# Attention blocks in an alternating order, a second bank for the filling, and probabilities turned as float32r

## The chip, the cores and the metric

The kernel runs on one core of a Trainium2 chip. The metric is the time of one execution on the device in microseconds, measured as a median over runs. A core has five engines with queues of their own: TensorE (PE in the profile, with PEld for its weight loads), VectorE (DVE), ScalarE (ACT), GpSimd (POOL) and SyncE (SP, which here issues nearly all DMA transfers). They run beside one another and wait for one another through semaphores. TensorE writes into PSUM, a memory of eight banks of 512 float32 values on each of 128 partitions.

## The reference

One step of a hybrid encoder layer: 1024 new frames of one stream (`x_prompt`) and 32 frames of a running stream with 512 cached frames (`x_sample`), both of width 1024. The input is normalised and projected to ten groups of columns. Two branches follow, causal attention with 16 heads of 64 and a forget bias, and a causal depthwise convolution over 31 frames with a layer norm. Each is gated and projected, the two are mixed by sigmoid gates, and a last projection and the residual close the layer. Everything is float32.

```
h = rmsnorm(x, norm_g)
q, k, v, logf, ga, ua, ub, gb, ma, mb = columns of h @ w_in      # q and k normalised per head
s = q @ k.T + (C[t] - C[s]);  C = cumsum(logf)                   # causal: masked above the diagonal
o = softmax(s) @ v
conv = dwconv(ua * sigmoid(ub)) + b_dw
ya = (o * silu(ga)) @ w_pa
yb = (silu(layernorm(conv)) * silu(gb)) @ w_pb
y = x + (sigmoid(ma) * ya + sigmoid(mb) * yb) @ w_out
```

It returns y for both streams, the new keys, values and log forget gates, and the tail of the convolution's input.

## The kernel before

**Layout.** Activations lie with channels on partitions and frames along the free axis: 1024 + 32 = 1056 columns, worked in three chunks of 352. A projection is computed as float32r products (`mms`, L97): weights and inputs are split into a high and a low part in float32r, and three products, high by high, low by high and high by low, are added in a bank. A tile of 128 output channels takes 3 chunks x 8 slices of the contraction x 3 products = 72 products of 352 columns. ScalarE casts the raw weights to the high part (`split_w`, L91), GpSimd subtracts for the low part (L94).

**Stages.** First the inputs are turned and split while the first projections start; then v, k, q and the two convolution inputs are projected, with the 31 taps of the convolution on VectorE (L258); then the gate ga. From about 591 to 1095 us lies the attention stage, on which every edit bears. After it come the projections of ya, yb and the output.

**The attention stage.** Queries are cut into 8 blocks of 128 frames per head. `Block.scores` (L894) computes the scores of block i against its (i + 1) x 128 keys, in one bank when there are up to 512 keys, in two otherwise (`nb`), with two products a bank: KB by QB (L905; high and low parts packed on 128 partitions) and KA by QA (L906; 68 partitions, with the forget bias in the last four). A product narrower than 256 columns is padded to 256 (`wm`), which touches block 0 alone. VectorE adds the causal mask on the diagonal (L908) and takes the row maximum (L910), ScalarE writes the exponential to a tile P in SBUF and sums the rows (L913), VectorE takes the reciprocal (L915), and GpSimd scales P in place (L916). The score bank is free again when the exponential is done.

`Block.turn` (L918) transposes P in tiles of 128 x 128 on TensorE (L926, 36 tiles a head, 576 in all): a product in which the tile of P is the stationary operand and the identity matrix the moving one, both float32. Up to four tiles share a bank `ptr` from the pool `psT`, and ScalarE or VectorE copies them to the tile pt (L929). When blocks 0 to 3, or 4 to 7, of a head are turned, `values` (L931) multiplies them by V (L940), and ScalarE and VectorE move the result to the tile ot (L945, L946), which is multiplied by the gate ga and stored for every second head.

**Filling.** Between the blocks TensorE works on projections that nothing in the stage needs: 22 chunk groups of gb, ma and mb (`gate_steps`, L747), 528 steps of three products each through one bank of the pool `pq`. ScalarE evacuates a finished chunk to a tile t (L753) and SP stores it (L754). Layer norm sums of the convolution branch (L978) and the blocks of the sample stream (class `Sample`) are fitted in as well.

**What sets the order.** On TensorE the order is that of the code (a manual schedule). The driver loop (from L1017) visits the blocks in the order 0 to 7 of each head; at a block n it issues the scores of block n + 3, the turn of block n, four filling steps, and the values of block n - 2 when they are due:

```
for n, b in enumerate(seq):
    if n + 3 < len(seq):
        start(seq[n + 3])
    ...
        b.turn()
        fill(4 if b.i > 2 or b.head.h != 8 else 0)
    if n >= 2 and pending(seq[n - 2]):
        seq[n - 2].values()
```

On the other engines a scheduler orders instructions; each engine, SP too, works through its own list in order, so an instruction that waits holds all behind it. A tile that is allocated again under its tag waits until the readers of the buffer's last content are done; `bufs` is the number of buffers of a tag. Before: scores have two buffers of two banks, `psT` three banks, the filling one. P has three buffers. The operands of a head, QA, QB, KA and KB, are loaded by SP in one burst of eight transfers (and V for every second head) five blocks ahead of the head's first block (`Head.load`, L767).

## Time and profile before

| what | us |
|---|---|
| median of 3 runs | 1403.2 |
| lowest and highest of them | 1402.51, 1405.59 |
| the profiled execution, as a run | 1405.11 |
| its span (first to last instruction) | 1403.3 |

The profile shows one execution. A row of busy time gives an engine's busy microseconds, its share of the span and its number of instructions. In a row of groups, the line, the engine, the operation and `output<-inputs` are followed by the count, the busy time in us and the mean of one in ns, and then by the engine's idle time just before them and what ended it. A row of the timeline has the start, the duration from the first start to the last end, and the instructions that it joins. Products are pipelined on PE: each row is longer than the distance to the next start, and it is that distance which counts. A row of windows gives the stretch, its length, the busy time of each engine, the granted TensorE clock, the share of the DMA engines and GB/s. A row of waits gives who waited, for whom, the sum in us, how often and the longest.

### The profile page before, as it was taken

What the parts mean: (1) busy time and instruction counts of PE and PEld (TensorE: products, weight loads), DVE (VectorE), ACT (ScalarE), POOL (GpSimd) and SP (SyncE); (2) the same over time, 40 slices, a digit from 0 to 9 for tenths busy, and PEclk for the clock granted to TensorE, in tenths of its full rate; (3) what the DMA queues carried; (4) which work ended last, traced back from release to release, by engine and by line L of the source; (5) the groups of instructions that cost most, each with busy time, mean ns of one, the idle gap of its engine ahead of it and who ended that gap; (6) DMA issues with size and microseconds to landing.
All of it is one profiled execution on the core that took longest, in us unless ns stands there. A gap on an engine that the chain in (4) does not pass through costs nothing.

```text
span 1403.3 us, 23422 instructions
## 1 busy us (share of the span) xinstructions
PE 1390.1 (99%) x8999; PEld 1303.6 (93%) x8999; DVE 866.0 (62%) x1199; ACT 604.2 (43%) x1180; POOL 617.5 (44%) x541
## 2 busy tenths in 40 slices
PE   8999999999999999999999999999999999999999
PEld 7999999999999999998888888878888999999998
DVE  6687787888898998646655656644444497132111
ACT  6322334646464642245454546544554455232100
POOL 2324254557585875343433433232332366254320
PEclk9999999999999999999999999999999999999999
DMA  4242333424342484335545546353532778444431
GB/s 181 92 141 92 119 108 99 160 76 142 106 152 92 138 194 150 111 100 129 148 107 160 146 136 177 101 154 109 155 115 73 276 254 271 143 138 142 150 108 47
DMA packets 102288, 192.77 MB, mean 137 GB/s; under 512 B 17248, under 2 KB 70368, under 8 KB 102176
## 3 DMA queue, kind: packets, MB, share of 16 engines
q1 hardware_dynamic: 102032, 191.21, 44.4%
q8 instruction: 71, 1.16, 0.4%
q14 instruction: 41, 0.34, 0.1%
q10 hardware_dynamic: 144, 0.07, 0.0%
HBM read 125.58 MB, written 65.64 MB: 136 GB/s over the span
## 4 chain that ended last, share of the span: by engine, by line
PE 92%; issue 3%; DVE 2%; ACT 2%; POOL 1%; DMA 1%; SPq 0%; ACTq 0%; POOLq 0%; DVEq 0%
PE pj L102 67%; PE pjv L582 7%; PE po L940 5%; PE ptr L926 4%; PE psS L905 3%; PE psS L906 2%; POOL wl L94 1%; PE pst L698 1%; PE pst L697 1%; PE po L885 0%; DVE y L1082 0%; PE ptx L427 0%; DMA xtok<-xt 0%; ACT xh L429 0%; PE pjs L541 0%
## 5 line engine op out<-in xcount | busy, mean ns | idle before, releaser
L102 PE MATMUL pj<-xh,wh 128*128 128x352 f32 (+2 forms) x1536 | 510.0, 332 | 1.7 <-ACT t L753 1.1
L102 PE MATMUL pj<-xh,wl 128*128 128x352 f32 (+2 forms) x1536 | 494.0, 322 | 1.9 <-POOL wl L94 1.9
L102 PE MATMUL pj<-xl,wh 128*128 128x352 f32 (+2 forms) x1536 | 495.5, 323 | 0.2
L94 POOL TENSOR_TENSOR wl<-raw,wh 128x384 fp32r<-128x384 f32 (+1 forms) x258 | 323.1, 1280 | 258.1 <-ACT wh L91 226.9
L258 DVE SCALAR_TENSOR_TENSOR y<-u,vec_t,y 128x1086 f32<-128x1086 f32 x240 | 382.5, 1594 | 23.7 <-ACT y L255 19.6
L102 PEld LDWEIGHTS pj<-xh,wh 128*128 128x128 f32 x1536 | 289.0, 188 | 10.2 <-ACT t L753 6.6
L102 PEld LDWEIGHTS pj<-xh,wl 128*128 128x128 f32 x1536 | 289.9, 189 | 2.5 <-POOL wl L94 2.2
L102 PEld LDWEIGHTS pj<-xl,wh 128*128 128x128 f32 x1536 | 289.1, 188 | 1.4 <-DVE xl L430 1.2
L916 POOL TENSOR_SCALAR P<-P,nm 128x128 f32<-128x128 f32 (+7 forms) x128 | 107.6, 842 | 283.3 <-DVE nm L915 216.9
L91 ACT CAST wh<-raw 128x1024 fp32r<-128x1024 f32 x86 | 90.1, 1048 | 111.2 <-PE pj L102 80.5
L913 ACT ACTIVATE P<-psS,nm 128x128 f32<-128x128 f32 (+7 forms) x128 | 95.4, 745 | 70.7 <-DVE nm L910 61.5
L910 DVE TENSOR_REDUCE nm<-psS 128x1 f32<-128x128 f32 (+7 forms) x128 | 96.8, 756 | 8.6
L908 DVE TENSOR_TENSOR psS<-psS,cmask 128x128 f32<-128x128 f32 x128 | 38.1, 297 | 100.3 <-PE psS L906 99.3
L929 ACT COPY pt<-ptr 128x512 f32<-128x512 f32 (+3 forms) x128 | 65.0, 508 | 75.8 <-PE ptr L926 75.1
L715 POOL TENSOR_TENSOR ql<-qn,qh 128x352 fp32r<-128x352 f32 (+1 forms) x48 | 66.0, 1374 | 68.0 <-ACT qh L714 54.9
L926 PE MATMUL ptr<-ident,P 128*128 128x128 f32 x576 | 84.2, 273 | 0.0
L940 PE MATMUL po<-pt,V 128*64 128x512 f32 (+1 forms) x384 | 75.8, 530 | 0.0
L926 PEld LDWEIGHTS ptr<-ident,P 128*128 128x128 f32 x576 | 69.1, 140 | 5.6 <-issue 0.4
L582 PE MATMUL pjv<-vwh,xh 128*128 128x260 f32 x256 | 72.5, 283 | 0.0
L582 PE MATMUL pjv<-vwl,xh 128*128 128x260 f32 x256 | 72.4, 283 | 0.0
L582 PE MATMUL pjv<-vwh,xl 128*128 128x260 f32 x256 | 72.3, 282 | 0.0
L905 PE MATMUL psS<-KB,QB 128*128 128x256 f32 (+2 forms) x192 | 70.1, 366 | 0.6 <-ACT t L751 0.6
(200 smaller groups left out, 2237.4 us busy)
## 6 DMA issues: line engine op xcount, KB each, us to landing
raw<-wf SPq DMA_DIRECT2D x88, 512.0 KB
QB<-s_q SPq DMA_DIRECT2D x32, 256.0 KB
KB<-s_k SPq DMA_DIRECT2D x32, 256.0 KB
kT<-qn SPq DMA_DIRECT2D x8, 528.0 KB
s_ga<-t SPq DMA_DIRECT2D x24, 176.0 KB
s_gb<-t SPq DMA_DIRECT2D x24, 176.0 KB
s_ma<-t SPq DMA_DIRECT2D x24, 176.0 KB
s_mb<-t SPq DMA_DIRECT2D x24, 176.0 KB
```

Of the source, the lines that this page charges most:

```text
L91: nc.scalar.copy(wh, raw)
L94: nc.gpsimd.tensor_sub(wl[:, k0:k1, :], raw[:, k0:k1, :], f32(wh[:, k0:k1, :]))
L102: nc.tensor.matmul(ps, a[:, kt, :], b(kt, sl), start=(first and n == 0), stop=(last and n == N - 1))
L258: t = nc.vector.scalar_tensor_tensor(y, u[:, i:i + CW], w, y, op0=ALU.mult, op1=ALU.add)
L582: nc.tensor.matmul(ps[:, :VC], a, b, start=(n == 0), stop=(n == 23))
L715: nc.gpsimd.tensor_sub(ql[:, :n], qn[:, o], f32(qh[:, :n]))
L905: nc.tensor.matmul(ps[:, b, :wm], QB[:, qsl], KB[:, ksl], start=True, stop=False)
L910: nc.vector.tensor_reduce(nm[:, 0:1], ps[:, :nb, :w], axis=AX.XY, op=ALU.max, negate=True)
L913: nc.scalar.activation(P[:, :nk].rearrange("p (b w) -> p b w", b=nb), ps[:, :nb, :w], AF.Exp, bias=nm[:, 0:1], accum_out=nm[:, 1:2])
L916: nc.gpsimd.tensor_scalar(P[:, :nk], P[:, :nk], nm[:, 2:3], 1.0, op0=ALU.mult, op1=ALU.mult)
L926: nc.tensor.transpose(pt[:, 128 * j:128 * j + 128], P[:, 128 * (4 * u + j):128 * (4 * u + j) + 128], ident)
L940: nc.tensor.matmul(po[64 * o:64 * o + 64, q0:], V[:, j + o, hd], p[:, j + o, q0:], start=(j == 0), stop=(j == njb - 2), skip_group_check=True)
```

## The change

The change has these parts:

- **Order.** A head's blocks run in the order 4, 0, 5, 1, 6, 2, 7, 3, so that a big block (two score banks) alternates with a small one (one bank). Scores are issued four blocks ahead in place of three, and values one block behind in place of two.
- **Banks.** Scores have one tile of two banks (tag S) and one of one bank (tag S1) in place of two tiles of two banks. The bank that this leaves is a second one for the filling (`pq2`); `Banks2` alternates between them.
- **Float32r turns.** P is split by size: tag P2 with two buffers for big blocks, P1 with one for small ones. After GpSimd's scaling, SP issues a transfer of P to a new tile R of type float32r (R2 with two buffers, R1 with one), and the turn reads R and an identity of type float32r, and writes the bank as float32r.
- **Padding.** Scores are no longer padded to 256 columns.
- **Loads.** The operands of a head are loaded two transfers a block, from eleven blocks ahead on. V has one buffer and is loaded when the values of blocks 0 to 3 of the head before are done. The gate tile ga is loaded with the values of blocks 4 to 7, and ot stored with those of blocks 0 to 3. The tile `shift` of the layer norm moves to the pool of the convolution's input.

```diff
 NWARM = 46
+ORDER = (4, 0, 5, 1, 6, 2, 7, 3)
+AHEAD = 4
 SAT = (2, 6, 10, 14)
...
     nc.vector.memset(eps_t, EPS)
-    ident = cp.tile([128, 128], F32, name="ident")
+    ident_r = cp.tile([128, 128], F32R, name="ident")
+    ident = f32(ident_r)
     smask = cp.tile([128, TS], F32, name="smask")
...
 
-    nc.vector.tensor_copy(ident, cst_t[:, C_ID:C_ID + 128])
+    nc.vector.tensor_copy(ident_r, cst_t[:, C_ID:C_ID + 128])
     u0 = u_tile(0)
...
 
-        def load(self):
+        def loads(self):
             h = self.h
-            self.q = [hp.tile([n, T], F32R, name=a, tag=a) for a, n in (("QA", 68), ("QB", 128), ("KA", 68),
-                                                                        ("KB", 128))]
-            QA, QB, KA, KB = self.q
+            self.q = QA, QB, KA, KB = [hp.tile([n, T], F32R, name=a, tag=a)
+                                       for a, n in (("QA", 68), ("QB", 128), ("KA", 68), ("KB", 128))]
             hs = slice(64 * h, 64 * h + 64)
-            nc.sync.dma_start(f32(QB[0:64]), s_q[1, hs, :])
-            nc.sync.dma_start(f32(QB[64:128]), s_q[0, hs, :])
-            nc.sync.dma_start(f32(KB[0:64]), s_k[0, hs, :])
-            nc.sync.dma_start(f32(KB[64:128]), s_k[1, hs, :])
-            nc.sync.dma_start(f32(QA[0:64]), s_q[0, hs, :])
-            nc.sync.dma_start(f32(QA[64:68]), s_aq[h])
-            nc.sync.dma_start(f32(KA[0:64]), s_k[0, hs, :])
-            nc.sync.dma_start(f32(KA[64:68]), s_ak[h])
-            if h % 2 == 0:
-                self.V = heads[h + 1].V = hp.tile([128, 8, 128], F32, name="V", tag="V")
-                nc.sync.dma_start(self.V, s_v[:, :, 64 * h:64 * h + 128].rearrange("b t d -> t b d"))
+            return [lambda d=d, a=a: nc.sync.dma_start(f32(d), a) for d, a in (
+                (KB[0:64], s_k[0, hs, :]), (KB[64:128], s_k[1, hs, :]), (QB[0:64], s_q[1, hs, :]),
+                (QB[64:128], s_q[0, hs, :]), (QA[0:64], s_q[0, hs, :]), (KA[0:64], s_k[0, hs, :]),
+                (QA[64:68], s_aq[h]), (KA[64:68], s_ak[h]))]
+
+        def load(self):
+            for fn in self.loads():
+                fn()
+            if self.h == 0:
+                self.load_v()
+
+        def load_v(self):
+            h = self.h
+            self.V = heads[h + 1].V = hp.tile([128, 8, 128], F32, name="V", tag="V", bufs=1)
+            nc.sync.dma_start(self.V, s_v[:, :, 64 * h:64 * h + 128].rearrange("b t d -> t b d"))
 
...
     cvt[0] = pool("cv7", 1, stack=p2, side="right")
-    taps.extend(last + sums(7))
-    psS = pool("psS", 2, stack=p2, space=PS)
+
+    def shift_again():
+        sides["shift"] = u7p.tile([128, UW], F32, name="u", tag="u")
+        nc.sync.dma_start(sides["shift"][:, :TT], s_m)
+        return 0.1
+
+    taps.extend(last + [shift_again] + sums(7))
+    psS = pool("psS", 1, stack=p2, space=PS)
     psT = pool("psT", 3, stack=p2, space=PS)
+    pq2 = pool("pq2", 1, stack=p2, space=PS)
+
+    class Banks2:
+
+        n = 0
+
+        def tile(self, *a, **k):
+            self.n += 1
+            return (pq, pq2)[self.n % 2].tile(*a, **k)
+
+    pF = Banks2()
     ap = pool("ap", 2, stack=p2, side="right")
...
         for n in range(NFILL):
-            yield from gate_steps(*fills.pop(0), pq)
+            yield from gate_steps(*fills.pop(0), pF)
 
...
             qsl = slice(i * 128, i * 128 + 128)
-            ps = psS.tile([128, 2, 512], F32, name="psS", tag="S")
             nb = 1 if nk <= 512 else 2
+            ps = psS.tile([128, nb, 512], F32, name="psS", tag="S" if nb == 2 else "S1")
             w = nk // nb
-            wm = max(w, 256)
             for b in range(nb):
-                ksl = slice(b * w, b * w + wm)
-                nc.tensor.matmul(ps[:, b, :wm], QB[:, qsl], KB[:, ksl], start=True, stop=False)
-                nc.tensor.matmul(ps[:, b, :wm], QA[:, qsl], KA[:, ksl], start=False, stop=True)
+                ksl = slice(b * w, b * w + w)
+                nc.tensor.matmul(ps[:, b, :w], QB[:, qsl], KB[:, ksl], start=True, stop=False)
+                nc.tensor.matmul(ps[:, b, :w], QA[:, qsl], KA[:, ksl], start=False, stop=True)
             diag = ps[:, nb - 1, w - 128:w]
...
             nc.vector.tensor_reduce(nm[:, 0:1], ps[:, :nb, :w], axis=AX.XY, op=ALU.max, negate=True)
-            self.P = P = ap.tile([128, T], F32, name="P", tag="P", bufs=3)
+            self.P = P = ap.tile([128, 512 * nb], F32, name="P", tag=f"P{nb}", bufs=nb)
             with tc.issue_after(sides["tables"].ins):
...
             nc.gpsimd.tensor_scalar(P[:, :nk], P[:, :nk], nm[:, 2:3], 1.0, op0=ALU.mult, op1=ALU.mult)
+            self.R = ap.tile([128, 512 * nb], F32R, name="R", tag=f"R{nb}", bufs=nb)
+            nc.sync.dma_start(f32(self.R[:, :nk]), P[:, :nk])
 
         def turn(self):
-            i, P = self.i, self.P
+            i, P = self.i, self.R
             pt_ = PT[i // 4]
...
                 for j in range(nj):
-                    nc.tensor.transpose(pt[:, 128 * j:128 * j + 128],
-                                        P[:, 128 * (4 * u + j):128 * (4 * u + j) + 128], ident)
+                    nc.tensor.transpose(pt[:, 128 * j:128 * j + 128].bitcast(F32R),
+                                        P[:, 128 * (4 * u + j):128 * (4 * u + j) + 128], ident_r)
                 put = nc.vector.tensor_copy if u else nc.scalar.copy
...
             if e == 1:
-                if c == 0:
+                if c == 1:
                     self.head.g = ap.tile([128, T], F32, name="ga", tag="kc", bufs=1)
...
                 nc.vector.tensor_mul(ot[:, osl], ot[:, osl], self.head.g[:, osl])
-            if e == 1 and c == 1:
-                nc.sync.dma_start(s_o[self.head.h // 2, :, :T], ot)
+                if c == 0:
+                    nc.sync.dma_start(s_o[self.head.h // 2, :, :T], ot)
+                    if self.head.h < H - 1:
+                        heads[self.head.h + 1].load_v()
 
...
     for h in heads:
-        seq += [Block(h, i) for i in range(8)]
+        seq += [Block(h, i) for i in ORDER]
         if h.h - 1 in SAT:
...
 
+    def first(b):
+        return getattr(b, "i", None) == ORDER[0]
+
     def start(b):
-        if getattr(b, "i", 1) == 0:
+        if first(b):
             h = b.head
...
 
-        shift = sides["shift"]
         for _ in range(4):
...
             nc.vector.scalar_tensor_tensor(rstd[:, sl], ps, 1.0 / D, t, op0=ALU.mult, op1=ALU.subtract)
-            nc.vector.tensor_add(mean[:, sl], mean[:, sl], shift[:, sl])
+            nc.vector.tensor_add(mean[:, sl], mean[:, sl], sides["shift"][:, sl])
             nc.vector.tensor_scalar(rstd[:, sl], rstd[:, sl], EPS, None, op0=ALU.add)
...
     ln = layernorm()
-    sides["shift"] = ap.tile([128, TT], F32, name="shift", bufs=1)
-    nc.sync.dma_start(sides["shift"], s_m)
+    loading = []
     start(seq[0])
     fill(8)
-    start(seq[1])
-    fill(4)
-    start(seq[2])
+    heads[1].load()
+    for b in seq[1:AHEAD]:
+        start(b)
+        fill(2)
     for n, b in enumerate(seq):
-        if n + 3 < len(seq):
-            start(seq[n + 3])
-        if n + 5 < len(seq) and getattr(seq[n + 5], "i", 1) == 0:
-            seq[n + 5].head.load()
-        if n + 6 < len(seq) and isinstance(seq[n + 6], Sample):
-            seq[n + 6].load()
+        if n + AHEAD < len(seq):
+            start(seq[n + AHEAD])
+        if n + AHEAD + 7 < len(seq) and first(seq[n + AHEAD + 7]):
+            loading.extend(seq[n + AHEAD + 7].head.loads())
+        for _ in range(2):
+            if loading:
+                loading.pop(0)()
+        if n + AHEAD + 3 < len(seq) and isinstance(seq[n + AHEAD + 3], Sample):
+            seq[n + AHEAD + 3].load()
         if isinstance(b, Sample):
...
             fill(4 if b.i > 2 or b.head.h != 8 else 0)
-        if n >= 2 and pending(seq[n - 2]):
-            seq[n - 2].values()
+        if n >= 1 and pending(seq[n - 1]):
+            seq[n - 1].values()
         if "ready" in sides:
             next(ln, None)
-    for b in seq[-2:]:
-        if pending(b):
-            b.values()
+    seq[-1].values()
     for _ in flow:
```

On TensorE the place is a block's scores, turn and first filling, in the middle of the stage. First before: the last score bank of block 5 (384 columns), then the turn of block 2 (three tiles) from P, which waits for GpSimd's scaling; `ptr` is a bank of psT.

```order
L905 MATMUL psS<-KB,QB 128x384
L906 MATMUL psS<-KA,QA 128x384
L926 MATMUL ptr_6902<-ident,P 128x128 [waits PE_49,Pool_49]
L926 MATMUL ptr_6902<-ident,P 128x128 x2
L102 MATMUL pj<-xh,wh 128x352
L102 MATMUL pj<-xh,wl 128x352
L102 MATMUL pj<-xl,wh 128x352
```

And now, the scores of block 2 and the turn of block 0:

```order
L927 MATMUL psS<-KB,QB 128x384
L928 MATMUL psS<-KA,QA 128x384
L950 MATMUL ptr_6940<-ident,R 128x128 [waits DMAHW7_49,Activation_49]
L104 MATMUL pj<-xh,wh 128x352
L104 MATMUL pj<-xh,wl 128x352
L104 MATMUL pj<-xl,wh 128x352
```

The turn reads R in place of P and waits for a transfer (DMAHW7 is one of the semaphores of SP's transfers) in place of GpSimd; a small block's scores now stand beside a small block's turn with a big block between it and the next.

On SP the place is a head's loads. Before, the stores of gates (s_ma), a raw weight, and the burst of loads for a head:

```order
L778 DMA V<-s_v 128x8x128 [waits DMAHW2_49,PE_49]
L85 DMA raw<-wf 128x1024 [waits DMAHW3_49,Activation_49,Pool_49]
L953 DMA s_o<-ot 128x1024 [waits DMAHW4_49,DVE_49]
L835 DMA kc<-ckT 128x2x512 [waits DMAHW5_49]
L768 DMA QB<-s_q 64x1024 [waits DMAHW6_49,PE_49]
L754 DMA s_ma<-t 128x352 [waits DMAHW7_49,Activation_49]
L769 DMA QB<-s_q 64x1024 [waits DMAHW0_49]
L770 DMA KB<-s_k 64x1024 [waits DMAHW1_49]
```

And now:

```order
L940 DMA R<-P 128x256 [waits DMAHW2_49,DMAHW7_49,PE_49,Pool_49]
L87 DMA raw<-wf 128x1024 [waits DMAHW3_49,Activation_49,Pool_49]
L940 DMA R<-P 128x896 [waits DMAHW4_49,Pool_49]
L757 DMA s_gb<-t 128x352 [waits DMAHW5_49,Activation_49]
L770 DMA KB<-s_k 64x1024 [waits DMAHW6_49,PE_49]
L940 DMA R<-P 128x384 [waits DMAHW2_49,PE_49,Pool_49]
L770 DMA KB<-s_k 64x1024 [waits DMAHW0_49]
L770 DMA QB<-s_q 64x1024 [waits DMAHW1_49]
```

The transfers of P to R stand among the stores of gates, the raw weights and the loads of a head; those of small blocks (128x256, 128x384) wait for GpSimd's scaling and for PE, that is for the turn that reads R before.

On ScalarE the place is a few exponentials and what is queued between them. Before:

```order
L929 COPY pt_6436<-ptr_7534 128x2x128 [waits PE_49]
L913 ACTIVATE P,nm<-psS,nm 128x640 [waits DVE_49,Pool_49]
L753 COPY t<-pj 128x352 [waits DMAHW1_49,PE_49]
L91 CAST wh<-raw 128x1024 [waits DMAHW4_49]
L929 COPY pt_6436<-ptr_7566 128x3x128 [waits PE_49]
L913 ACTIVATE P,nm<-psS,nm 128x768 [waits DVE_49,Pool_49]
```

And now:

```order
L935 ACTIVATE P,nm<-psS,nm 128x896 [waits DMAHW1_49,DVE_49]
L969 COPY ot<-po 64x512 [waits PE_49]
L953 COPY pt_6439<-ptr_7266 128x128 [waits PE_49]
L935 ACTIVATE P,nm<-psS,nm 128x384 [waits DMAHW1_49,DVE_49,Pool_49]
L953 COPY pt_6440<-ptr_7305 128x4x128 [waits PE_49]
L756 COPY t<-pj 128x352 [waits DMAHW7_49,PE_49]
L953 COPY pt_6439<-ptr_7343 128x2x128 [waits PE_49]
```

The exponential, which waited for VectorE and GpSimd, now waits for a transfer as well, since the tile P that it writes is read by the transfer to R; behind it in the queue stand the copies of turned tiles (L953), the evacuation of the filling (L756) and the values (L969).

2 lines of the change are left out of this document (1 added, 1 removed).

## The prediction

> **What bounds the kernel now.** The first view is the page's table of busy time, the second the table of busy time by stretch, laid over the attention stage, since every edit sits between the start of that stage and the projections behind it.
>
> ```profile
> PE 1390.1 (99%) x8999; PEld 1303.6 (93%) x8999; DVE 866.0 (62%) x1199; ACT 604.2 (43%) x1180; POOL 617.5 (44%) x541
> 591.00:1095.00 504.00, 501.59 (x3256) 427.08 (x3256) 268.13 (x589) 246.59 (x542) 179.01 (x206) 1.00 0.46 130
> ```
>
> TensorE (PE) is busy 99% of the span. In the attention stage it works 501.59 of 504.00 us at a granted clock of 1.00, while VectorE and ScalarE are busy about half of it; DMA engines are busy 0.46 and move 130 GB/s. The view of waits, for PE from 575 to 1095 us, says what is left to remove:
>
> ```profile
> PE pj L102 <- POOL wl L94: 1.9, 1, 1.9
> PE pj L102 <- ACT t L753: 1.1, 2, 0.8
> PE psS L905 <- ACT t L751: 0.6, 1, 0.6
> ```
>
> The first number is microseconds in total. Only 3.6 us are waits, and only the middle row (the filling's one bank waits for its evacuation) is one that the second bank can remove. So PE's stream sets the end: whatever shortens a PE instruction here shortens the kernel, and whatever makes PE wait lengthens it one for one. A reordering by itself gains nothing.
>
> **The turns as float32r.** The timeline of PE around one block gives the spacing of each kind of instruction (start, busy time, count):
>
> ```profile
> 872.67 0.39 PE L905 MATMUL psS<-KB,QB 128*128 128x256 f32 x1
> 872.90 0.28 PE L906 MATMUL psS<-KA,QA 68*128 68x256 f32 x1
> 873.02 0.93 PE L926 MATMUL ptr<-ident,P 128*128 128x128 f32 x7
> ...
> 875.70 0.34 PE L905 MATMUL psS<-KB,QB 128*128 128x384 f32 x1
> 875.88 0.34 PE L906 MATMUL psS<-KA,QA 68*128 68x384 f32 x1
> 876.05 1.04 PE L926 MATMUL ptr<-ident,P 128*128 128x128 f32 x8
> 876.85 0.40 PE L102 MATMUL pj<-xh,wh 128*128 128x352 f32 x1
> 877.09 0.32 PE L102 MATMUL pj<-xh,wl 128*128 128x352 f32 x1
> ```
>
> Eight turns end 1.04 us after the first began and one alone is 0.27 us long (the groups below), so they are (1.04 - 0.27) / 7 = 0.110 us apart; seven give (0.93 - 0.27) / 6 = 0.110 too. The groups of the stage count them:
>
> ```profile
> L926 PE MATMUL ptr<-ident,P 128*128 128x128 f32 x576 | 84.2, 273 | 0.0
> L926 PEld LDWEIGHTS ptr<-ident,P 128*128 128x128 f32 x576 | 69.1, 140 | 5.6 <-issue 0.4
> ```
>
> 576 x 0.110 = 63.4 us of PE. No turn in float32r is in the trace, so the new price is bounded. From below by the column rate of float32r products: this row of the chain has 24 of 352 columns in 3.82 us.
>
> ```profile
> 225.31 3.82 PE pj L102 x24
> ```
>
> One is 3.82 / 24 = 0.159 us, 0.45 ns a column, and 128 columns are 0.058 us. From above, unless the rival further down holds, by the weight load, since a turn's stationary operand is the block of P itself. Two kinds of load are seen, in the timeline of weight loads at the kernel's start:
>
> ```profile
> 19.65 0.31 PEld L427 LDWEIGHTS ptx<-ident,xtok 128*128 128x128 f32 x3 [1.67 <-DVE xl L430]
> 19.93 0.19 PEld L102 LDWEIGHTS pj<-xh,wh 128*128 128x128 f32 x1
> 20.04 0.19 PEld L102 LDWEIGHTS pj<-xh,wl 128*128 128x128 f32 x1
> ```
>
> Three turn loads fit in 0.31 us, so with 0.14 for one they are (0.31 - 0.14) / 2 = 0.085 apart; loads of float32r products are 0.11 apart. If a float32r turn loads as a turn does, it costs 0.058 to 0.085 us; if as a float32r product does, 0.11, which is no gain at all. I take 0.065, near the column rate, because the loads of PEld lie beside PE's products: 576 x (0.110 - 0.065) = **-25.9 us**, bounds -29.9 and 0.
>
> The Trainium skill, page "TensorE: Matmul & The Clock Gate", section "LDWEIGHTS (loading the stationary operand)", prices a load by its columns alone, about 107 ns for 128. The float32r rows at 0.11 agree with it and the turn loads at 0.085 do not; by that rule this term would be 0.
>
> **The unpadded scores.** Only block 0 was padded: 16 heads x 2 products x 128 columns fewer x 0.45 ns = **-1.9 us**. A bound on the other side is in the rival on narrow float32r.
>
> **The second bank for filling** takes away the 1.1 us wait: **-1.1 us**, bounds -1.1 and 0. The order of blocks, the spread head loads and the earlier values leave PE's count of other products as it was: 0 by themselves.
>
> **The new transfers and single buffers.** 128 transfers P to R join SP's queue, after the work of POOL and ahead of every turn. They hold 16 heads x 36 tiles of 64 KB = 37.7 MB, 75 GB/s over 504 us on top of 130, so the DMA share should go from 0.46 to about 0.46 x 205 / 130 = 0.72. Small blocks (up to 512 keys) now have one P, one R and one score bank, so a new ring appears: a turn of small block k ends, SP issues R of the next small block, it lands, P comes free, the exponential of the small block after that runs, the bank comes free, and the scores of the following small block, which PE meets two blocks later, may start. The rows for the ring:
>
> ```profile
> 885.01 0.32 SPq L754 DMA_DIRECT2D s_ma<-t  x1
> L913 ACT ACTIVATE P<-psS,nm 128x512 f32<-128x512 f32 x16 | 11.0, 689 | 15.2 <-DVE nm L910 13.9 <-POOL P L916 0.8 <-DVE nm L915 0.3
> L913 ACT ACTIVATE P<-psS,nm 128x384 f32<-128x384 f32 x16 | 9.4, 585 | 3.2 <-DVE nm L910 2.7
> L913 ACT ACTIVATE P<-psS,nm 128x128 f32<-128x128 f32 x16 | 6.1, 382 | 2.3 <-DVE nm L910 2.3
> L913 ACT ACTIVATION_READ_ACCUMULATOR P<-psS,nm 128x1 f32 x128 | 25.1, 196 | 0.0
> ```
>
> PE's time between the two ends of the ring is its own work: 12 filling products are 12 x 0.159 + 0.08 (the first one after turns is 0.24 from the next, above, instead of 0.16) = 2.0 us, a score pair of a bank is 2 x 0.45 ns a column, a turn 0.065.
> - Turn of block 1 to scores of the next head's block 0: 2.0, then the next head's block 4 scored (4 x 320 columns, 0.6), block 6 turned (7, 0.5), 2.0: 5.1 us. The ring needs 0.32 to issue and 0.69 + 0.20 for the exponential of block 3, which leaves the transfer 3.9 us.
> - Turn of block 2 to the next block 1: 2.0 + 0.7 (4 x 384) + 0.5 + 2.0 = 5.2; less 0.32 and 0.38 + 0.20, 4.3 us.
> - Turn of block 0 to block 3: 2.0 + 0.9 (4 x 512) + 0.4 + 2.0 = 5.3; less 0.32 and 0.59 + 0.20, 4.2 us.
> - Turn of block 3 to the next block 2 lies across both sets of values and has over 9 us: nothing.
>
> How long a transfer takes to land, these rows bound: one that SP waited for on an idle queue, two that the chain shows in crowded stretches.
>
> ```profile
> SPq L1243 <- DMA yT<-xres: 1.4, 1, 1.4
> 1185.52 3.72 DMA s_ya<-sma
> 1.18 4.84 DMA xtok<-xt
> ```
>
> At 1.4 and at 3.72 every ring closes in time. At 4.84 on all of them the three come 0.94 + 0.54 + 0.64 = 2.1 us late a head, 34 us over 16 heads. While an exponential waits, ScalarE's queue behind it stands too: copies of turned blocks, evacuations of the filling, the casts of weights; and while SP waits for P or R, the stores of gates and the loads of weights and heads wait behind. I take a third of 34, **+12 us**, since a share of 0.72 on average means that some stretches are full; bounds 0 and +34.
>
> Big blocks have P and R twice, so only their single score tile is new. It is emptied by a maximum and an exponential:
>
> ```profile
> L910 DVE TENSOR_REDUCE nm<-psS 128x1 f32<-128x1024 f32 x16 | 19.6, 1224 | 1.1
> L913 ACT ACTIVATE P<-psS,nm 128x1024 f32<-128x1024 f32 x16 | 17.9, 1118 | 12.3 <-DVE nm L910 9.2 <-PE pj L102 2.9
> L916 POOL TENSOR_SCALAR P<-P,nm 128x1024 f32<-128x1024 f32 x16 | 18.0, 1126 | 37.6 <-DVE nm L915 32.6 <-DMA QB<-s_q 5.1
> ```
>
> 1.2 + 1.1 + 0.2 = 2.5 us after the scores, against some 5 us of PE's work until the next big block's scores: 0. The turn itself now waits for R: from block 7's scores 2.5 us, then POOL's 1.1, 0.32 to issue and the transfer, 7.8 us with 3.72 for it, 8.9 with 4.84. Four blocks ahead PE has four times 2.0 us of filling and the blocks' own scores and turns between, some 11 us: 0. SP issues 128 x 0.32 = 41 us more in 504: 0, as long as it waits in no ring.
>
> **Sum.** -25.9 - 1.9 - 1.1 + 12 = -16.9 us. The profiled execution itself took 1405.1 us (span 1403.3, 1.8 around it): 1405.1 - 16.9 = 1388.2. The median of the runs shown is 1403.2, 1.9 below that execution, so the forecast is **1386 us**. With every term at its good end it is 1403.2 - 29.9 - 3 = 1370.
>
> **Rivals.**
> *The ring of the small blocks closes late.* This is the other side: slower with turns as cheap as forecast. What the edits win is 28.9 us, 1.8 a head; the three waits together are 3L - 12.4 us a head for a transfer time L, so the sign turns at L = 4.7 us. For it speaks that the slack is 0.2 us over 3.72, and that one transfer of 4.84 stands above; against it, that a transfer of one block of at most 256 KB is smaller than most others, and that the DMA engines are not full. At L = 5.0 the waits are 2.6 x 16 = 42: 1403.2 + 13 = 1416 us; at 4.84, 1408.
> *The turn doesn't get cheaper.* It is held at 0.11 us by float32r loads, and the change does not do what it says. For it: the rows 0.11 apart; against: the turn loads 0.085 apart. Then the turns give 0, the rest -3.0; PE's work between the ends of the rings is 0.3 us longer, so the waits are nearer 8: 1403.2 - 3 + 8 = 1408 us, 1400 with no waits and 1437 with 34 and no other gain.
> *Float32r narrower than 256 columns runs at the full float32 pace.* The old code pads its scores to 256, and no float32r product below 256 columns is in the trace. A plain float32 product costs two instructions at the pace of a turn (0.110 for 128), 0.22 us: the turns lose 576 x 0.11 = 63 us, and the waits vanish in the longer work: 1403.2 + 63 = 1466 us. For it only the padding; against it, that a turn does no arithmetic to split.
>
> **Chances.** Cheap turns 0.54, of which the late ring takes 0.12 (slower, about 1410), the band within 0.2% 0.03, and the forecast side 0.39. Turns held at 0.11: 0.28, of which faster 0.05, within 0.2% 0.06, slower 0.17. Slow narrow products 0.15, slower. Anything else 0.03, faster, 0.01 within it. Within 0.2% means within 2.8 us of 1403.2, about what a measurement of this kernel can tell from no change. Faster 0.46, same 0.10, slower 0.44. The likeliest single case is the forecast, with its own range from 1370 to 1400; faster and slower hold nearly the same, so the range must reach over the late ring and the held turns to 1432, and leaves out the slow narrow products (0.15) and the far tail.
>
> **What would show it.** In PE's timeline, turns 0.058 to 0.07 us apart prove the main term, 0.11 the second rival, 0.22 the third. The window that covers the attention stage should shrink from 504 to some 487 us with a DMA share near 0.72; the stages ahead and behind should stay. In PE's waits, psS scores that wait for the exponential, or turns that wait for a transfer of R, summing to about 12 us, prove the ring's price; over 29 us they turn the sign; and ScalarE's waits for P's transfer, behind which they stand, should name R. The wait of the filling for its evacuation should be gone. If the stage loses PE time without the turns getting closer, or if the waits are of PE for weights (stores and loads late behind R on SP), my account is wrong.

## The result, and the profile after

The change made the kernel slower: 1464.95 us (median of 6 runs, 1463.17 to 1476.79) against 1402.86 (6 runs, 1401.71 to 1405.59), a ratio of 1.0458, 95% interval 1.0439 to 1.0478. The forecast was 1386, and the range ended at 1432. The profiled execution took 1476.79 with a span of 1474.7; it is the slowest of the six. The values of attention now end at 1167 us in place of 1095: the loss lies in the attention stage.

The first line is the busy time of the page of the changed kernel, the rows below it are busy times by stretch of 100 us in its attention stage (stretch, length, PE, PEld, DVE, ACT, POOL, granted clock, DMA share, GB/s).

```profile
PE 1407.0 (95%) x8999; PEld 1312.6 (89%) x8999; DVE 869.8 (59%) x1199; ACT 600.3 (41%) x1180; POOL 624.9 (42%) x541
600.00:700.00 100.00, 88.77 (x543) 77.33 (x543) 53.22 (x107) 43.64 (x95) 39.95 (x38) 0.93 0.61 174
700.00:800.00 100.00, 90.33 (x560) 75.15 (x559) 51.51 (x102) 39.85 (x89) 34.62 (x33) 0.93 0.61 175
800.00:900.00 100.00, 89.79 (x577) 74.06 (x575) 50.22 (x106) 44.43 (x99) 35.62 (x37) 0.95 0.68 192
900.00:1000.00 100.00, 84.76 (x488) 69.89 (x490) 49.45 (x122) 43.71 (x102) 27.72 (x34) 0.91 0.70 190
1000.00:1100.00 100.00, 89.31 (x576) 76.78 (x573) 38.31 (x92) 40.44 (x93) 25.23 (x33) 0.95 0.63 185
```

PE is idle a tenth of the stage, where it was idle for 2.4 us in 504, and the clock, 1.00 before, is 0.91 to 0.95: 7 + 7 + 5 + 9 + 5 = 33 us of full-speed work are lost to it at most, 29 if only the time is counted in which PE was working. The view of PE's waits from 591 to 1170 us names what it stands for:

```profile
PE ptr L950 <- DMA R<-P: 33.2, 15, 4.2
PE psS L927 <- ACT P L935: 22.8, 16, 3.2
PE psS L871 <- ACT P L935: 0.8, 1, 0.8
```

57 us, of which 33 are turns that wait for their transfer and 24 are scores whose bank is held by an exponential. What holds the exponentials, and what SP's transfers of P wait for, stands in the waits of ScalarE and of SP from 600 to 1100 us:

```profile
ACT P L935 <- DMA R<-P: 104.3, 41, 6.4
SPq L940 <- PE ptr L950: 50.6, 24, 8.0
```

The chain of waits shows one such place (start, us, what):

```profile
806.84 8.50 DMA R<-P
815.33 0.02 issue
815.35 0.02 ACTq L935
815.37 0.04 issue
815.41 0.47 ACT P L935 x2
815.88 0.04 issue
815.93 0.58 PE psS L927
```

A transfer of 256 KB took 8.5 us, P came free, the exponential ran, the bank came free, the scores ran: the ring of the prediction, with a landing almost twice its longest. A few microseconds earlier a big block's turn waits for its own R. PE's timeline, and the stretches of a microsecond around it:

```profile
807.19 0.33 PE L928 MATMUL psS<-KA,QA 68*128 68x384 f32 x1
810.66 1.23 PE L950 MATMUL ptr<-ident,R 128*128 128x128 f32 x8 [3.14 <-DMA R<-P]
811.69 0.62 PE L104 MATMUL pj<-xh,wh 128*128 128x352 f32 x1
812.11 0.49 PE L104 MATMUL pj<-xh,wl 128*128 128x352 f32 x1
812.40 0.49 PE L104 MATMUL pj<-xl,wh 128*128 128x352 f32 x1
```

```profile
808.00:809.00 1.00, 0.00 (x0) 0.00 (x0) 0.93 (x1) 0.00 (x0) 0.00 (x0) 1.00 1.14 213
809.00:810.00 1.00, 0.00 (x0) 0.00 (x0) 0.00 (x0) 0.00 (x0) 0.00 (x0) 0.95 0.97 197
810.00:811.00 1.00, 0.34 (x3) 0.37 (x3) 0.00 (x0) 0.00 (x0) 0.00 (x0) 0.50 1.07 221
...
815.00:816.00 1.00, 0.61 (x3) 0.16 (x2) 0.09 (x2) 0.46 (x2) 0.00 (x0) 0.50 0.84 322
816.00:817.00 1.00, 1.00 (x7) 1.00 (x8) 1.00 (x2) 0.00 (x0) 0.84 (x1) 0.63 0.35 135
817.00:818.00 1.00, 1.00 (x8) 1.00 (x8) 0.90 (x3) 0.59 (x1) 0.56 (x1) 1.00 0.02 6
```

After 3.14 us of standing still the filling products are 0.29 us apart (812.11 to 812.40) in place of 0.16, and the granted clock is 0.50 from just before 810 to past 816: this wait of 3.1 us cost about 3 more behind it. The DMA engines are full while PE waits (1.14, 0.97, 1.07). The Trainium skill, page "TensorE: Matmul & The Clock Gate", section "Part 1: The HAM clock gate", says that TensorE's clock is halved when it has been idle for a window of about 3.4 us and comes back after as much work. The trace agrees in kind, but not on the length of the idle time; here the clock fell some 2.4 us into the wait and stayed low for nearly 7 us. In the attention stage of this trace the granted clock stood at 0.50 thirteen times, seven times for 3.41 us and six times for 6.83. Each of the five waits of over 3 us was followed by 6.83 us of it, and a wait of 1.76 us (at 701.40) was still followed by 3.41.

Why R lands late is in the trace too. For each transfer of R from 600 to 1110 us I took the time from the start of SP's issue to the last completion signal, and counted the transfers that SP had issued before it and that had not landed when its own issue ended:

```
not yet landed ahead    0     1     2     3     4     5     6     7
transfers of R         12    34    16     8    11    12    12    10
mean us to landing    2.5   3.3   3.8   4.8   6.8   7.0   7.7   7.8
```

The median is 4.5, one in ten takes over 8.3, the longest 11.0. In the 9.3 us from 798.98 to 808.28, SP issued KB twice, QB twice, QA and KA (256 KB each), a raw weight (512 KB) and the transfers of four blocks.

### The profile page after: what moved, and what is told of

The parts are those of the page before. It is cut to its first block, busy times and chain, and to the rows that moved or that the text cites. A ratio compares the mean times of both kernels' runs of the same rounds, so it can differ in the third digit from the quotient of the medians.

```text
span 1474.7 us, 23716 instructions
## 1 busy us (share of the span) xinstructions
PE 1407.0 (95%) x8999; PEld 1312.6 (89%) x8999; DVE 869.8 (59%) x1199; ACT 600.3 (41%) x1180; POOL 624.9 (42%) x541
## 4 chain that ended last, share of the span: by engine, by line
PE 76%; DMA 12%; issue 3%; DVE 3%; ACT 3%; POOL 2%; SPq 1%; ACTq 0%; POOLq 0%; DVEq 0%
PE pj L104 57%; DMA R<-P 11%; PE pjv L585 6%; PE po L964 5%; PE psS L927 2%; PE ptr L950 2%; PE psS L928 1%; POOL wl L96 1%; POOL P L938 1%; ACT P L935 1%; DMA QB<-s_q 1%; PE pst L701 1%; PE pst L700 0%; PE po L908 0%; SPq L770 0%
## 5 line engine op out<-in xcount | busy, mean ns | idle before, releaser
L104 PE MATMUL pj<-xl,wh 128*128 128x352 f32 (+2 forms) x1536 | 502.7, 327 | 0.2 <-DVE xl L433 0.2
L104 PE MATMUL pj<-xh,wl 128*128 128x352 f32 (+2 forms) x1536 | 501.4, 326 | 0.4 <-POOL wl L96 0.4
L938 POOL TENSOR_SCALAR P<-P,nm 128x640 f32<-128x640 f32 (+7 forms) x128 | 118.6, 928 | 348.1 <-DVE nm L937 340.5
L935 ACT ACTIVATE P<-psS,nm 128x640 f32<-128x640 f32 (+7 forms) x128 | 95.0, 742 | 155.2 <-DMA R<-P 111.6
L950 PEld LDWEIGHTS ptr<-ident,R 128*128 128x128 f32 x576 | 63.5, 146 | 42.6 <-issue 32.7
L950 PE MATMUL ptr<-ident,R 128*128 128x128 f32 x576 | 69.4, 252 | 33.2 <-DMA R<-P 33.2
L932 DVE TENSOR_REDUCE nm<-psS 128x1 f32<-128x640 f32 (+7 forms) x128 | 96.5, 755 | 7.7 <-DVE psS L930 0.5
L953 ACT COPY pt<-ptr 128x512 f32<-128x512 f32 (+3 forms) x128 | 64.6, 505 | 86.5 <-PE ptr L950 85.4
L937 DVE RECIPROCAL nm<-nm 128x1 f32<-128x1 f32 x128 | 20.7, 162 | 133.1 <-ACT P L935 132.9
L927 PE MATMUL psS<-KB,QB 128*128 128x384 f32 (+1 forms) x192 | 73.8, 386 | 23.7 <-ACT P L935 22.8
L927 PEld LDWEIGHTS psS<-KB,QB 128*128 128x128 f32 x192 | 37.5, 195 | 43.7 <-ACT P L935 30.1
```

What stands on the lines that cost most here:

```text
L104: nc.tensor.matmul(ps, a[:, kt, :], b(kt, sl), start=(first and n == 0), stop=(last and n == N - 1))
L927: nc.tensor.matmul(ps[:, b, :w], QB[:, qsl], KB[:, ksl], start=True, stop=False)
L932: nc.vector.tensor_reduce(nm[:, 0:1], ps[:, :nb, :w], axis=AX.XY, op=ALU.max, negate=True)
L935: nc.scalar.activation(P[:, :nk].rearrange("p (b w) -> p b w", b=nb), ps[:, :nb, :w], AF.Exp, bias=nm[:, 0:1], accum_out=nm[:, 1:2])
L938: nc.gpsimd.tensor_scalar(P[:, :nk], P[:, :nk], nm[:, 2:3], 1.0, op0=ALU.mult, op1=ALU.mult)
L950: nc.tensor.transpose(pt[:, 128 * j:128 * j + 128].bitcast(F32R), P[:, 128 * (4 * u + j):128 * (4 * u + j) + 128], ident_r)
```

## The experiments

Theory A: the cost is that PE waits for transfers that land late among the loads of heads, directly and through the ring, and that the clock falls behind the waits. Rivals: B, the order, the banks or the single buffers stall PE by themselves; C, the turns do not get cheaper; D, the traffic itself slows the stage; E, it is bandwidth and not the queue that makes R late.

| run | what differs from the changed kernel | median us | ratio to before, 95% |
|---|---|---|---|
| e1 | GpSimd writes R, no transfer | 1391.1 | 0.9912 (0.9898 to 0.9927) |
| e2 | turns from P as float32, no R | 1400.2 | 0.9976 (0.9967 to 0.9985) |
| e3 | e1 and idle transfers into one tile | 1437.5 | 1.0246 (1.0229 to 1.0263) |
| e4 | the kernel before, P as float32r | 1394.2 | 0.9936 (0.9921 to 0.9951) |
| f1 | heads 2 to 15 load no q and k | 1398.2 | 0.9967 (0.9957 to 0.9977) |
| f2 | R issued by ScalarE | 1482.1 | 1.0564 (1.0538 to 1.0590) |
| f3 | two small R | 1474.7 | 1.0496 (1.0469 to 1.0524) |
| f4 | e1 and idle transfers to DRAM | 1397.9 | 0.9960 (0.9946 to 0.9974) |
| g1 | e1 and R transferred on to DRAM | 1390.6 | 0.9906 (0.9891 to 0.9921) |
| g2 | loads one for each block | 1499.5 | 1.0683 (1.0664 to 1.0702) |
| g3 | only big blocks by transfer | 1443.9 | 1.0281 (1.0263 to 1.0298) |
| g4 | only small blocks by transfer | 1449.1 | 1.0313 (1.0286 to 1.0341) |

**e1: without the transfers.**

```diff
-            nc.gpsimd.tensor_scalar(P[:, :nk], P[:, :nk], nm[:, 2:3], 1.0, op0=ALU.mult, op1=ALU.mult)
             self.R = ap.tile([128, 512 * nb], F32R, name="R", tag=f"R{nb}", bufs=nb)
-            nc.sync.dma_start(f32(self.R[:, :nk]), P[:, :nk])
+            nc.gpsimd.tensor_scalar(self.R[:, :nk], P[:, :nk], nm[:, 2:3], 1.0, op0=ALU.mult, op1=ALU.mult)
```

> The changed kernel without its 128 transfers: GpSimd writes the scaled probabilities straight into R as float32r (so they are rounded to float32r, which the changed kernel's copy does not do). Order, banks, single small buffers and float32r turns stay. Theory A (the transfers land late behind the loads of heads, and the ring of single small buffers turns that into waits of PE, after which the clock is granted at half): no wait of PE of more than 5 us in sum, granted clock 1.00 in the stage, and the turns' price 576 x (0.110 - 0.073) = 21 us, the scores' 2 and the bank's 1 come through: 1403 - 24 = 1379 us, 1374 to 1386. Rival B (one score tile per size or the order itself makes PE wait, with or without transfers): 1420 us or more. Rival C (the order costs nothing, but the turns do not get cheaper): 1396 to 1404.

1391.1 us, 73.9 below the changed kernel, with the same order, banks and single buffers. PE's waits from 591 to 1160 us:

```profile
PE psS L927 <- ACT P L935: 2.3, 2, 1.4
PE psS L871 <- ACT P L935: 2.1, 2, 1.3
```

B falls: the transfers make the whole loss. But 1391 is 5 us above theory A's range, since the turns bring less than 21. The 0.073 of the expectations is near the mean distance between the starts of turns inside a block (0.077 us in e1); what counts is the time up to the filling, which the next two experiments price.

**e2 and e4: what a turn costs.** e2 takes R away and turns P (`bufs=2 * nb`) with `ident` as float32. e4 is the kernel before with P as a float32r tile that ScalarE and GpSimd write:

```diff
-    ident = cp.tile([128, 128], F32, name="ident")
+    ident_r = cp.tile([128, 128], F32R, name="ident")
+    ident = f32(ident_r)
...
-            self.P = P = ap.tile([128, T], F32, name="P", tag="P", bufs=3)
+            self.P = P = ap.tile([128, T], F32R, name="P", tag="P", bufs=3)
...
-            nc.gpsimd.tensor_scalar(P[:, :nk], P[:, :nk], nm[:, 2:3], 1.0, op0=ALU.mult, op1=ALU.mult)
+            nc.gpsimd.tensor_scalar(P[:, :nk], f32(P)[:, :nk], nm[:, 2:3], 1.0, op0=ALU.mult, op1=ALU.mult)
...
-                    nc.tensor.transpose(pt[:, 128 * j:128 * j + 128],
-                                        P[:, 128 * (4 * u + j):128 * (4 * u + j) + 128], ident)
+                    nc.tensor.transpose(pt[:, 128 * j:128 * j + 128].bitcast(F32R),
+                                        P[:, 128 * (4 * u + j):128 * (4 * u + j) + 128], ident_r)
```

> The changed kernel without R: P has two buffers for small and four for big blocks, and the turns read P as float32, as before. Order, banks, unpadded scores and spread loads stay. Theory A: 1403 - 2 (scores) - 1 (bank) = 1400 us, 1396 to 1405, no waits. Rival B (order or banks): 1420 or more. The difference to the kernel with GpSimd writing R prices the turns: 21 us if a float32r turn takes 0.073, 0 if the spacing of 0.073 in the changed kernel was bought elsewhere.

> The kernel before with one thing changed: the exponential and GpSimd write P as float32r (rounded twice), and the turns read it as float32r; no transfer, old order, old banks, padded scores. Theory A: the turns alone, 576 x (0.110 - 0.073) = 21 us: 1382 us, 1377 to 1388, turns 0.073 us apart. Rival C (the turn is not cheaper where PE has no pauses): 1400 to 1404.

e2 is 3.0 us below before (1400.2 against 1403.2), what scores and bank were to bring. The float32r turns bring 9.1 in the new order (1400.2 to 1391.1) and 9.0 in the old one (1403.2 to 1394.2): both runs agree on a price, and the 21 of the expectation was wrong. PE's timeline in e4 shows a block of eight:

```profile
896.67 0.79 PE L927 MATMUL ptr<-ident,P 128*128 128x128 f32 x8
897.29 0.40 PE L102 MATMUL pj<-xh,wh 128*128 128x352 f32 x1
897.53 0.32 PE L102 MATMUL pj<-xh,wl 128*128 128x352 f32 x1
```

From the first turn to the second filling product are 0.86 us, where before it was 1.04 (876.05 to 877.09). Over all blocks the median of this stretch is 0.867 for eight turns and 0.528 for four, so each further turn costs 0.085 us, not 0.065, and for a single turn it is 0.278 in both kernels. Summed over the eight blocks the medians fall by 0.68 us a head, 11 in all, near the 9 that were measured (in e4, PE's waits for the evacuation of the filling grew from 1.1 to 3.7 us). 0.085 is the distance at which turn loads stand in the trace of before: that the load holds the turn is likely, but only argued.

**e3 and f4: traffic without anyone waiting, two misses.** Both add to e1, at the place of each transfer, one of the same size from a constant tile: e3 into one tile D, f4 to 16 places in DRAM. e3 also takes the second buffer of P from the big blocks.

```diff
-            self.P = P = ap.tile([128, 512 * nb], F32, name="P", tag=f"P{nb}", bufs=nb)
+            self.P = P = ap.tile([128, 512 * nb], F32, name="P", tag=f"P{nb}", bufs=1)
...
+            D = ap.tile([128, T], F32, name="D", tag="D", bufs=1)
+            nc.sync.dma_start(D[:, :nk], f32(xh[:, 0, :nk]))
```

> As the kernel with GpSimd writing R as float32r, but SP also issues, at the place of each former transfer, one of the same size from a constant input tile to a tile that nobody reads (one buffer, so each waits for the one before; P has one buffer per size). The 37.7 MB and the places in SP's queue stay, no engine waits for them. Theory A (only the waiting for them costs): within 8 us of the kernel without transfers, 1379 to 1388, clock 1.00. Rival D (the traffic itself slows PE or its loads, or lowers the granted clock): 1410 or more, with a granted clock below 0.97 in the stage.

> GpSimd writes R as float32r (rounded), and SP issues at the place of each former transfer one of the same size from a constant input tile to one of 16 scratch places in DRAM that nobody reads, so that neither engine nor buffer waits for it. It separates the traffic from SP standing still, which the run with one target tile mixed. Theory A (only waiting for the transfers costs): 1391 to 1400, no wait of PE over 3 us, clock 1.00. Rival D (the traffic itself costs, by late loads or a lower clock): 1415 or more.

e3 gave 1437.5, far from its 1379 to 1388. PE's waits say what it measured:

```profile
PE psS L871 <- DMA kc<-ckT: 25.1, 3, 12.2
PE psS L927 <- ACT P L935: 9.9, 6, 2.9
```

The one tile D made SP wait for each landing before the next (213 us in all), and the loads of the sample stream stood behind it. In f4 nothing depended on the transfers, and they were all issued in the first 160 us. The kernel was 7 us slower than e1, and the loss lies there: in the first 70 us PE was busy for 60.40 us in place of 66.05, at a clock of 0.95 in place of 1.00, with a DMA share of 0.96 (347 GB/s) in place of 0.40 (137 GB/s), and one wait of 5.2 us for a split input. What made that input late was not followed. Neither run says what traffic does in the attention stage.

**g1: the traffic in its place.** e1, and SP transfers R on, after GpSimd wrote it:

```diff
+            nc.sync.dma_start(s_d[(8 * self.head.h + i) % 16, :, :nk], f32(self.R[:, :nk]))
```

> The transfers that nobody read had been moved by the scheduler to another stage, so their traffic was not in the attention stage. Now GpSimd writes R as float32r, and SP transfers R itself, after it is written, to one of 16 scratch places in DRAM; PE reads R and waits for no transfer, but R's buffer is held until its transfer has landed. Traffic in place without PE behind it: theory A (waiting is what costs) 1391 to 1405, waits of PE under 12 us, clock 0.99 or more. Rival D (traffic costs by itself, late loads or a lower clock): 1420 or more.

1390.6 us, the same as e1. The stretch from 600 to 1100 us:

```profile
600.00:1100.00 500.00, 494.84 (x3317) 423.51 (x3316) 276.76 (x603) 254.05 (x553) 171.49 (x202) 1.00 0.68 215
```

215 GB/s and a DMA share of 0.68, more than the changed kernel moves, at a clock of 1.00 and with PE as busy as in e1. D falls for this stage: this traffic costs nothing unless PE waits for it (it goes to DRAM, though, where the changed kernel's goes to SBUF). R's buffers were held by it all the same, as the waits of GpSimd from 591 to 1160 us show:

```profile
POOL R L940 <- DMA s_d<-R: 74.5, 18, 7.6
```

A buffer that waits for a landing is thus not enough either; here the wait ended before it reached PE.

**f1: without the loads of heads.**

```diff
         def loads(self):
             h = self.h
+            if h > 1:
+                self.q = heads[h - 2].q
+                return []
```

> The changed kernel, but heads 2 to 15 load no q and k and compute with those of heads 0 and 1 (the outputs of attention are then not the reference's; the work of every engine but the 112 loads is the same). Transfers to R, rings and buffers stay. Theory A (R lands late because it queues behind the loads of heads: in the changed kernel it lands 2.5 us after its issue begins with nothing ahead of it and 7 to 8 us with four or more transfers ahead): PE's waits for R and for the exponential fall from 57 us to under 12, clock above 0.99, near the 1391 of the kernel without transfers plus those waits: 1391 to 1405. Rival B (the single buffers cannot close in time even with a quick transfer): 1435 or more.

1398.2 us with all transfers to R, rings and single buffers in place. PE's waits, and the stretch from 600 to 1100 us:

```profile
PE psS L930 <- ACT P L938: 9.2, 10, 1.4
600.00:1100.00 500.00, 489.56 (x3263) 414.50 (x3262) 270.10 (x593) 245.37 (x544) 184.45 (x198) 1.00 0.46 164
```

R now lands in 2.9 us at the median, 4.5 at the ninetieth percentile. So 67 of the 74 us need the loads of heads beside the transfers.

**f2: another queue.** `nc.scalar.dma_start` in place of `nc.sync.dma_start` for R.

> The changed kernel with the transfers to R issued by ScalarE in place of SP. Bytes, rings and buffers stay; R no longer stands in SP's list, and if ScalarE's transfers have a queue of their own in the DMA engines, it no longer lies behind the loads of heads there either. Theory A with queueing as the cause: R lands in 2 to 4 us, waits of PE below 25 us, 1400 to 1430, held up by ScalarE waiting for GpSimd. Rival E (the engines' bandwidth is the limit, in whatever queue): R still lands at 4 to 8 us, 1450 or more.

1482.1 us. The DMA queues from 600 to 1100 us (packets, MB, share) and PE's waits:

```profile
q1 hardware_dynamic: 29927, 57.84, 41.8%
q10 hardware_dynamic: 16005, 32.82, 21.2%
```

```profile
PE ptr L950 <- DMA R<-P: 32.4, 12, 5.0
PE psS L927 <- ACT P L935: 21.6, 19, 2.0
PE psS L871 <- ACT P L935: 9.6, 3, 4.7
```

R went through q10, a queue of its own, and landed as late as before: 4.2 us at the median, 7.7 on average with seven transfers of both queues under way. E's forecast came, and a queue of its own did not help. That the transfers share the DMA engines, whatever their queue, fits this; it was not separated from other causes.

**f3: two small R.** `bufs=2` for R of small blocks, `t352("t", 2)` and `bufs=3` for nm.

> The changed kernel with two buffers of R for small blocks in place of one (room from two in place of three tiles for evacuations, three in place of six for row maxima). Then the transfer of a small block no longer waits for the turn of the one before. If the ring of the small blocks is what turns late landings into waits: the waits for the exponential (22.8 us) go to under 8, SP's waits for the turn (50.6 us) go, the loads bunch less, and the time falls by 20 to 45 us to 1420 to 1445. If late landings hurt the turns in any case: less than 15 us, 1450 to 1465.

1474.7 us, no gain. SP no longer waits for turns, but for GpSimd, and PE waits as long:

```profile
PE ptr L950 <- DMA R<-P: 34.0, 15, 5.3
PE psS L927 <- ACT P L935: 12.8, 8, 3.2
PE psS L871 <- ACT P L935: 6.4, 2, 3.3
```

Less for exponentials, the same for turns, and a time above both forecasts. The ring through R alone does not make the loss; but the run also took buffers from the evacuations and the row maxima, so it does not price that ring.

**g3 and g4: which blocks.** R by transfer where nb is 2 (g3) or 1 (g4), by GpSimd otherwise.

```diff
+            to = P if nb == 2 else self.R
+            nc.gpsimd.tensor_scalar(to[:, :nk], P[:, :nk], nm[:, 2:3], 1.0, op0=ALU.mult, op1=ALU.mult)
+            if nb == 2:
+                nc.sync.dma_start(f32(self.R[:, :nk]), P[:, :nk])
```

> Only blocks of more than 512 keys get R by a transfer (26 of 36 tiles); small blocks get it from GpSimd, rounded. The ring of single small buffers then holds no transfer. If the ring of the small blocks makes the waits: 1391 to 1410. If late landings hurt big blocks as much (their turns wait for R): the waits of turns for R stay near the 33 us of the changed kernel and the time is 1430 to 1455.

> The reverse: only blocks of up to 512 keys get R by a transfer (10 of 36 tiles); big blocks get it from GpSimd, rounded. If the small ring makes the waits: the waits for the exponential stay near 20 us, less a little for the 27 MB that go, and the time is 1415 to 1450. If it takes the full traffic to make R late: 1391 to 1405.

First PE's waits in g3, then in g4:

```profile
PE ptr L952 <- DMA R<-P: 32.7, 14, 5.3
PE psS L927 <- ACT P L935: 2.3, 2, 1.4
```

```profile
PE psS L927 <- ACT P L935: 34.8, 21, 3.7
PE psS L871 <- ACT P L935: 8.0, 4, 3.8
```

There are two paths, and each is enough: big blocks' turns wait for R (53 us over e1), small blocks' ring waits for P (58 us over e1). The turns' 32.7 us in g3 are those of the changed kernel, as the second case of its expectation said; the 42.8 us in g4 are twice the 20 that were expected. The two paths together make 74, less than the sum of the two runs, presumably because a stop on the one gives the other time.

**g2: loads really apart.** One load for each block, behind that block's R on SP, begun one block earlier.

```diff
...
+                with tc.issue_after(sides["R"].ins):
+                    loading.pop(0)()
...
```

> The changed kernel with the loads of a head really apart: one for each block, each held behind that block's transfer to R in SP's list, begun one block earlier, the last three (one of 256 KB, two of 16 KB) together. Bytes, rings and buffers stay. If the bunch of loads is what makes R late: R lands in 2.5 to 4.5 us nearly always, waits of PE below 20 us, clock 0.99, 1398 to 1420. If the sum of traffic is too much whatever its order: 1450 or more.

1499.5 us, a miss in the other direction. PE's waits:

```profile
PE psS L928 <- DMA KA<-s_ak: 31.0, 8, 5.9
PE psS L928 <- DMA KA<-s_k: 27.3, 5, 6.8
PE psS L927 <- ACT P L935: 15.4, 12, 2.6
```

R landed in 3.8 us at the median and 6.5 at the ninetieth percentile, sooner than the 4.5 and 8.3 of the changed kernel. Turns no longer wait for it, but scores wait for their operands: a load behind an R on SP waits for whatever that R waits for (SP stood 101 us for turns). Whether loads that are apart and not held by R would do is not settled; it was not tried.

**Waits and clock make up the time.** For each profiled execution whose waits grew: PE's waits in the stage for transfers and exponentials (in e3 one of 3.9 us for VectorE too) beyond e1's 4.4 us, and what the clock took, against the span beyond e1's 1390.4. The clock's share is half of the time in which PE worked at a granted clock of 0.50, summed over the trace of the stage; time in which PE stood still anyway is not counted again.

| run | waits | clock | sum | span beyond e1 |
|---|---|---|---|---|
| the changed kernel | 52.4 | 29.3 | 81.7 | 84.3 |
| e3 | 34.5 | 11.6 | 46.1 | 44.0 |
| f1 | 5.3 | 0.0 | 5.3 | 7.1 |
| f2 | 59.2 | 22.0 | 81.2 | 86.8 |
| f3 | 48.8 | 32.3 | 81.1 | 83.9 |
| g2 | 75.7 | 33.6 | 109.3 | 109.6 |
| g3 | 32.7 | 14.8 | 47.5 | 47.2 |
| g4 | 38.4 | 14.1 | 52.5 | 56.3 |

No run kept the waits and spared the clock, so this split is arithmetic, but it closes within 6 us in eight kernels, and g1, with the most traffic and none of these waits beyond e1's, has a clock of 1.00.

## Why the prediction was wrong, step by step

- **What bounds the kernel** was right: PE's stream set the end before, and each wait that the change added lengthened it.
- **Scores and second bank**, -1.9 and -1.1: the sum was right. e2 gives -3.0 together, and PE no longer waits for the filling's evacuation; the two were not measured apart.
- **The turns**, -25.9: the sign was right, the size was not. Measured -9, so this term is 17 of the 79 us between forecast and result. The value of 0.065 was chosen near the column rate, "because the loads of PEld lie beside PE's products"; the spacing is 0.085, the end of the range that came from the turn loads, and the first turn of a block gains nothing. The Trainium skill, page "TensorE: Matmul & The Clock Gate", section "LDWEIGHTS (loading the stationary operand)", would have it at about 0.107 and no gain: the runs do not agree with that for turns.
- **The new transfers and single buffers**, +12: the step that failed. It measured +73.9 (1391.1 to 1465.0); with -9.1 and -3.0 that is the whole +61.8 from 1403.2. It failed in three parts. First, the landing time was bounded at 4.84 us by rows from the kernel's start and its last stage, and a third of the sum was taken because of a mean DMA share; in the stage itself it is 4.5 at the median and up to 11. The share was near 1 where R was late (0.97 to 1.14 around 809) while its mean was 0.65, and f1 shows that the loads of heads are what makes it late. Loads that land late were there to be seen before: QA's took 5.5 to 7.6 us in the old trace's bursts. Second, "the turn itself now waits for R ... 0" compared 8.9 us with 11; a landing of 8 us uses that up, and the 33 us of waiting turns, as dear as the ring, had no term (g3, with this path alone, loses 53 us over e1). Third, the granted clock was taken as given; behind each wait of over 3 us it was halved for 6.83, and by the table it makes 29 of the 84 us.
- **The rivals.** The late ring is one half of what happened, and its place was right (ScalarE waits 104.3 us for R's transfers, as the prediction said it would); priced at 1408 to 1416, it lacked the turns' path and the clock. The slow narrow products had the closest time, 1466, by accident: float32r turns are 0.085 apart, not 0.22.
- **DMA share**, forecast 0.72: 0.61 to 0.70. **SP's issues** at no cost "as long as it waits in no ring": it waited in one, 51 us for turns.

## What to carry to other kernels

A copy between a producer and an engine that never waits puts the landing time of a transfer on that engine's path: price it by the slowest landings in the same stage, with all that is in flight, and not by an idle queue or a mean share. Traffic that PE did not wait for was free in this stage, even where a buffer was held until it landed (g1); the same traffic was not, where the operand of the next turn or the tile of the next exponential hung on it. And here the producer could write the type itself, rounded, which beats both kernels (1391 us). Where TensorE is the bound, a wait of 3 us or more is to be counted for up to about twice its length, because of the clock behind it: in the changed kernel each of the five was followed by 6.83 us at half the clock, in g3 and g4 some by 3.41.

## What had not been expected of the hardware

- The granted clock fell to 0.50 about 2.4 us into a wait of 3.14 us and stayed there for 6.83 us, with the products 0.29 us apart in place of 0.16. In this stage of the changed kernel it stayed there for 3.41 us or 6.83 us and for no other time.
- A queue of its own did not bring R in sooner: 4.2 us at the median through q10 against 4.5 through q1.
- A further float32r turn of a block costs 0.085 us beside 0.110 in float32, a quarter less and not half, and a block's first turn gains nothing.
